# A planned encoder kernel: POOL held to the planned order on its shared SBUF path, later landings in the plan, and a last pass by token tiles

## The chip, the cores and the metric

The kernel runs on one core of a Trainium2 chip. The metric is the device time of one execution in microseconds; the median of three runs stands for a kernel. Engines are named as the profile names them: PE (TensorE), DVE (VectorE), ACT (ScalarE), POOL (GpSimd), SP (SyncE, which issues every DMA here).

## What is computed

A post-norm encoder layer over two sequences, a prompt of 512 tokens and a sample of 1024, width 1024. In float32:

```python
def encoder_layer(x, ...):
    h = x @ w_in                                              # 1024 -> 2048
    c_val, c_gate, r_x, r_gate = split(h, 4)                  # 512 channels each
    c = c_val * sigmoid(c_gate)
    c = silu(layer_norm(depthwise_conv(c, width=31)))         # centred
    rec = (rg_lru(depthwise_conv(r_x, width=4, causal), forward)
           + rg_lru(depthwise_conv(r_x, width=4, anti), reverse)) * gelu(r_gate)
    x = layer_norm(ALPHA * x + concat(c, rec) @ w_out)
    u = depthwise_conv(x @ w_up, width=3)                     # 1024 -> 2 * 2816
    val, gate = split(u, 2)
    f = (gelu(gate) * val) @ w_down                           # 2816 -> 1024
    return layer_norm(ALPHA * x + f)

def encoder_trunk(x, ...):                                    # both sequences
    return encoder_layer(layer_norm(x), ...)
```

`rg_lru` is a gated linear recurrence along the sequence (two small gate products, sigmoid, exp, sqrt, a scan).

## The kernel before

**Products in three terms.** Every product is made of float32r halves: an operand is split into a rounded high part (a copy, mostly on ACT) and a low part (the difference, a TENSOR_TENSOR), and `prod3` multiplies high by high, high by low and low by high. So each weight tile costs a load, an ACT copy and a subtraction on DVE or POOL before PE can use all of it; the low parts of weights that are used again are stored to DRAM and loaded the next time (`weight`).

**Stages.** The prompt and the sample are normed and projected (`ln_in`, `w_in_p`, `w_in_s`). Then a mixer (31-tap convolution and recurrences, work for DVE, ACT and POOL) runs beside a feed-forward pass of another block (work for PE): `mixer_p` beside `w_in_s`; `mixer_s(1)` (second half of the sample) beside `ffn(None)` (prompt), about 360 to 720 us; `mixer_s(0)` beside `ffn(1)`, about 800 to 1040 us; at last `ffn(0)` alone. A feed-forward pass goes over 22 pairs of 128-channel tiles: `up(p)` makes both tiles of a pair, evaluates the 3-tap convolution, gelu and product, and splits the result into one of two buffers `fb`; `down` multiplies a group of pairs by w_down into two PSUM banks in turn (U3 and M2, slot names), and each bank is added to the page `y` by one DVE instruction before PE may write it again. The groups are `GROUPS`: one pair, five times three, two, four.

**Layer norm.** `ln_stats` makes the statistics on DVE and 1/sqrt(var + eps) with one POOL instruction (pow, 128x1, line 197). In the mode "act" a DVE instruction (128x1) makes -mean/std, ACT normalizes, and two TENSOR_TENSOR of 128x1024 apply gain and bias on DVE or POOL ("any"); in the mode "dve" two SCALAR_TENSOR_TENSOR of 128x1024 do all of it.

**What sets the order.** No order is written by hand. Every operation is recorded with reads, writes, an assumed cost and a priority, and `Sched.emit` makes a plan: it lists operations engine by engine, taking at each point the one with the best priority that can start, and the program then issues them in that order. Each engine works through its own queue strictly in that order, waiting by semaphores for data only. For operations marked "any" the plan chooses DVE or POOL. The plan knows that a POOL instruction that reads SBUF and a DVE instruction with two SBUF inputs exclude each other (`takes_port`, `port`), but nothing in the program holds the engines to that: POOL starts when its data is there. A load is planned to be usable when its bytes have passed a modelled bus.

**The last pass, `ffn(0)`.** All pairs but the last are issued in the loop. `last` then issues the last pair's `up`, and the first two token tiles of the last group start with the pairs that are ready and are closed when the last pair is. `body` goes on with token tile 0 and 1 (closing products), a correction row for one page of the other block (`E0`, `a5s`), and tiles 2 and 3; each is normed and stored as 128x1024.

## Time and profile before

| | |
|---|---|
| median of 3 runs | 1616.22 us (1615.35 to 1616.29) |
| the profiled execution | 1616.81 us, of which its span is 1615.0 us |
| PE busy | 1556.7 us, 96% of the span |
| DVE, ACT, POOL busy | 1200.4, 820.3, 188.1 us |
| chain that ended last, by engine | PE 50%, DVE 26%, ACT 10%, DMA 9%, issue 4% |
| matmuls of 128x512 | 6724, 1532.1 us busy in all |

PE is busy nearly all the time, so the time splits into PE's work and the stretches in which PE stands: before its first large product, in short stops in between, and after its last one. A table by stage shows where they are; the stops are read one by one from PE's timeline, and what PE waited for from the table of waits.

### The profile page before, as it was taken

The page shows a single profiled execution, that of the slowest core. Times are in us where ns is not written, and L with a number is a line of the kernel's source. Part 1 is how long each engine was busy: PE and PEld are TensorE (multiplying, and loading weights), DVE is VectorE, ACT ScalarE, POOL GpSimd, SP SyncE. Part 2 cuts the span into 40 slices and gives each one's busy share as a digit, 9 for nine tenths or more (in the row PEclk, how much of TensorE's full clock was granted, in tenths as well). Part 3 has the DMA queues.
Part 4 walks back from the last instruction along what each step waited for, and adds up shares of the span by engine and source line. Part 5 has one row for each costly group of instructions (what it writes and reads, how often), then busy time and mean ns, then how long its engine had stood idle before and what let it go on. Part 6 is the DMA issues. An engine that isn't in the chain of part 4 may idle for free.

```text
span 1615.0 us, 19015 instructions
## 1 busy us (share of the span) xinstructions
PE 1556.7 (96%) x7012; PEld 1281.2 (79%) x7012; DVE 1200.4 (74%) x1867; ACT 820.3 (51%) x1019; POOL 188.1 (12%) x159
## 2 busy tenths in 40 slices
PE   5999999999999999999999999999999999999996
PEld 5887888887778777788888878788887888888784
DVE  8999995498989999873689899844438644545448
ACT  3737775148687974344359833352424433333341
POOL 3102121002122222010101100000001000000003
PEclk9999999999999999999999999999999999999998
DMA  9862335466567455657686676476665556555541
GB/s 359 299 219 96 126 118 187 165 208 206 158 193 223 153 189 190 202 169 248 204 259 201 214 251 202 160 253 200 195 212 196 195 194 195 202 183 195 184 162 65
DMA packets 107517, 316.09 MB, mean 196 GB/s; under 512 B 11936, under 2 KB 12064, under 8 KB 107296
## 3 DMA queue, kind: packets, MB, share of 16 engines
q1 hardware_dynamic: 107424, 314.88, 58.8%
q8 instruction: 55, 0.90, 0.2%
q14 instruction: 38, 0.31, 0.1%
HBM read 247.72 MB, written 67.11 MB: 195 GB/s over the span
## 4 chain that ended last, share of the span: by engine, by line
PE 50%; DVE 26%; ACT 10%; DMA 9%; issue 4%; SPq 0%; POOL 0%; DVEq 0%; ACTq 0%; POOLq 0%
PE b L258 48%; DVE b L206 15%; DVE b L197 9%; ACT b L236 7%; DMA b<-w_up 6%; ACT L236 3%; PE b L266 1%; DMA b<-mixs_d 1%; DMA b<-w_down 1%; DVE b L708 1%; DMA lo_in_d<-b 1%; DVE b L413 0%; DMA b<-lo_out_d 0%; DMA b<-xp 0%; SPq L247 0%
## 5 line engine op out<-in xcount | busy, mean ns | idle before, releaser
L258 PE MATMUL b<-b,b 128*128 128x512 f32 (+1 forms) x6724 | 1532.1, 389 | 24.5 <-DVE b L197 15.9
L258 PEld LDWEIGHTS b<-b,b 128*128 128x128 f32 x6724 | 1247.8, 189 | 293.6 <-DVE b L197 26.5
L206 DVE SCALAR_TENSOR_TENSOR b<-b,b,b 128x511 f32<-128x511 f32 (+12 forms) x848 | 593.0, 715 | 177.5 <-ACT b L236 156.6
L236 ACT ACTIVATE b<-b 128x1024 fp32r<-128x1024 f32 (+4 forms) x576 | 447.3, 799 | 533.6 <-PE b L258 197.2
L197 DVE TENSOR_TENSOR b<-b,b 128x512 f32<-128x512 f32 (+6 forms) x483 | 396.0, 840 | 122.8 <-ACT b L236 70.4
L236 ACT ACTIVATE b<-b,b 128x512 f32<-128x512 f32 (+1 forms) x337 | 256.9, 784 | 220.9 <-PE b L258 160.3
L197 POOL TENSOR_TENSOR b<-b,b 128x1 f32<-128x1 f32 (+3 forms) x89 | 113.6, 1282 | 674.1 <-DVE b L220 443.7
L236 ACT ACT_TABLE_LOAD x106 | 136.0, 1283 | 26.7 <-DVE b L206 23.9
L197 POOL TENSOR_TENSOR b<-b 128x512 f32<-128x512 f32 x52 | 73.3, 1409 | 609.1 <-ACT b L236 597.6
L206 DVE SCALAR_TENSOR_TENSOR b<-b,b 128x512 f32<-128x512 f32 (+2 forms) x81 | 53.6, 673 | 62.5 <-PE b L258 61.8
L413 DVE BATCH_NORM_STATS2 b<-b 128x6 f32<-128x512 f32 x84 | 56.7, 688 | 12.1 <-PE b L266 6.7
L197 DVE TENSOR_TENSOR b<-b 128x512 f32<-128x512 f32 (+3 forms) x80 | 46.5, 600 | 25.8 <-ACT b L236 24.9
L206 DVE SCALAR_TENSOR_TENSOR b<-b 128x512 f32<-128x512 f32 (+1 forms) x110 | 56.0, 518 | 6.8 <-POOL b L197 3.4
L266 PE MATMUL b<-b,b 128*128 128x128 f32 x288 | 40.0, 281 | 17.9 <-DVE b L206 12.1
L266 PEld LDWEIGHTS b<-b,b 128*128 128x128 f32 x288 | 34.8, 145 | 23.9 <-DVE b L206 10.7
L708 DVE TENSOR_TENSOR_SCAN b<-b 128x512 f32<-128x512 f32 x24 | 29.3, 1223 | 0.7
L1046 POOL MEMSET b<- 128x128 f32 x1 | 0.2, 207 | 134.6 <-PE b L258 134.6
L220 DVE TENSOR_SCALAR b<-b 128x1 f32<-128x1 f32 (+1 forms) x61 | 10.3, 171 | 1.7
L415 DVE BATCH_NORM_AGGREGATE b<-b 128x2 f32<-128x12 f32 (+1 forms) x48 | 9.5, 199 | 0.9
L243 DVE COPY b<-b 128x2 f32<-128x2 f32 x44 | 6.6, 150 | 0.0
L220 DVE TENSOR_SCALAR b<-b,b 128x512 f32<-128x512 f32 x2 | 0.9, 484 | 0.0
L900 POOL MEMSET b<- 128x1 f32 x8 | 0.3, 99 | 1.0 <-PE b L258 1.0
(11 smaller groups left out, 1.6 us busy)
## 6 DMA issues: line engine op xcount, KB each, us to landing
b<-w_up SPq DMA_DIRECT2D x132, 512.0 KB, 4.4
b<-lo_up_d SPq DMA_DIRECT2D x88, 512.0 KB, 4.2
b<-w_down SPq DMA_DIRECT2D x132, 256.0 KB, 4.0
lo_up_d<-b SPq DMA_DIRECT2D x44, 512.0 KB, 5.1
b<-lo_down_d SPq DMA_DIRECT2D x88, 256.0 KB, 3.5
b<-w_in SPq DMA_DIRECT2D x32, 512.0 KB, 5.2
b<-w_out SPq DMA_DIRECT2D x24, 512.0 KB, 4.4
lo_down_d<-b SPq DMA_DIRECT2D x44, 256.0 KB, 5.3
```

Of the source, the lines that this page charges most:

```text
L197: return self.op(eng, cost if eng == "any" else cost[eng], lambda e=eng: self.engine(e).tensor_tensor(out=out(), in0=a(), in1=b(), op=op), ...
L206: o = self.op("dve", cost, lambda: self.nc.vector.scalar_tensor_tensor(out=out(), in0=a(), scalar=s() if isinstance(s, View) else s, in1=b ...
L220: return self.op(eng, cost, lambda: e.tensor_scalar(out=out(), in0=a(), scalar1=f(s1), scalar2=f(s2), op0=op0, **({"op1": op1} if op1 is n ...
L236: self.nc.scalar.activation(out=out(), in_=a(), func=func, **k)
L243: return self.op("dve", cost, lambda: self.nc.vector.tensor_copy(out(), a()), [a], [out], prio)
L258: self.nc.tensor.matmul(out=out(), lhsT=a(), rhs=b(), start=start and i == 0, stop=stop and i == len(pairs) - 1)
L266: self.nc.tensor.transpose(o(), i(), ident())
L413: S.op("dve", c.n * 1.0417 + 69, lambda i=i, c=c: nc.vector.bn_stats(out=sm_[6 * i:6 * i + 6](), in_=c()), [c], [sm_[6 * i:6 * i + 6]], prio)
L415: S.op("dve", 211, lambda: nc.vector.bn_aggr(out=sm_[12:14](), in_=sm_[0:6 * n]().rearrange("p (a b) -> p a b", a=n)), [sm_[0:6 * n]], [sm ...
L708: S.op("dve", out.n * 2.0833 + 69, lambda: nc.vector.tensor_tensor_scan(out=out(), data0=a(), data1=b(), initial=0.0, op0=ALU.mult, op1=AL ...
L900: S.op("pool", 100, lambda z=z: nc.gpsimd.memset(z.f32(), 0.0), [], [z], ev)
L1046: S.op("pool", 200, lambda: nc.gpsimd.memset(E0.all.f32(), 0.0), [], [E0.all], 60)
```

## The change

Six edits. (1) The plan remembers which DVE operation took the shared path last (`holder`); a POOL operation that takes it next gets a semaphore wait on that DVE operation (`add_manual_dep`), and in the plan it is ready only a signal's time after it. This concerns 105 POOL instructions; where another wait of POOL already implies it, no wait is added in the program. (2) A load counts as landed 1.4 us later in the plan (`LAND`). (3) The instruction that makes -mean/std moves from DVE to POOL (37 of them, TENSOR_SCALAR). (4) `ffn(0)` has three buffers `fb` in place of two; all 22 pairs are issued in the loop; the last two groups are left to the end. (5) The last group is finished token tile by token tile, eight banks in turn. (6) The last token tile is normed and stored in halves of 128x512. Since the plan is made anew, the order of all engines moves a little everywhere.

```diff
+LAND = 1400.0
-        port = 0.0
+        port, holder = 0.0, None
...
         def ready_on(o, e):
             rt = o.rt.get(e, 0.0)
-            return max(rt, port) if takes_port(o, e) else rt
+            if not takes_port(o, e):
+                return rt
+            return max(rt, port + (LAT["dve", "pool"] if e == "pool" and holder is not None else 0.0))
...
             if takes_port(o, e):
                 port = t + cost
+                if e == "pool":
+                    o.after = holder
+                holder = o if e == "dve" else None
             if e == "sp":
                 bus = max(bus, t + 1500) + o.nbytes / 360.0
-                o.end = bus
+                o.end = bus + LAND
...
         for o in order:
-            if o.both:
-                o.fn(o.eng)
-            else:
-                o.fn()
+            o.ins = o.fn(o.eng) if o.both else o.fn()
+            if o.after is not None:
+                self.tc.add_manual_dep(o.ins.ins, o.after.ins.ins.name, mybir.DependencyInfo(
+                    mybir.DependencyClass.Sync, mybir.DependencyReason.DATA), reason="port")
...
-            S.stt(s_[16:17], mean, -1.0, rstd, ALU.mult, ALU.mult, prio)
+            S.ts("pool", s_[16:17], mean, rstd, ALU.mult, -1.0, ALU.mult, prio=prio - 1.5)
...
-        fb = [S.buf("A0", [2, 2, 512], f32r), S.buf("A1", [2, 2, 512], f32r)]
+        fb = [S.buf(n, [2, 2, 512], f32r) for n in (("A0", "A1", "GB") if blk == 0 else ("A0", "A1"))]
...
+        late = len(GROUPS) - (2 if blk == 0 else 1)
         for gi, grp in enumerate(GROUPS):
             for p in grp:
-                if blk == 0 and p == NPAIR - 1:
-                    break
                 up(p)
-            if gi < len(GROUPS) - 1:
+            if gi < late:
                 down(gi, grp)
...
+            down(late, GROUPS[late], None, PR + 0.2105)
+            wdslot = rot(["G2", "A5", "GW", "A6"])
+            return wds(grp), grp, products
...
     for i in range(4):
         for nh in range(2):
-            b = bank[nh, i]
-            S.mm(b.all, products(get, nh, i, grp[-1:] if i < 2 else grp), i >= 2, True, 70.21 + 0.01 * i)
+            b = S.buf(names(), [512], psum=True)
+            S.mm(b.all, products(get, nh, i, grp), True, True, 70.22 + 0.01 * i)
             yv = y0[i // 2][i % 2, nh * 512:(nh + 1) * 512]
             S.tt("dve", yv, yv, b.all, ALU.add, 6)
...
+    s_ = sm("s")
+    mean, rstd = ln_stats(page_of(y0[1], 1)["halves"], s_, 5.5)
+    for nh in range(2):
+        c = slice(nh * 512, (nh + 1) * 512)
+        x = y0[1][1, c]
+        S.stt(x, x, mean, gb2b[0].buf[0, c], ALU.subtract, ALU.mult, 6)
+        S.stt(x, x, rstd, gb2b[0].buf[1, c], ALU.mult, ALU.add, 6)
+        S.dma(lambda c=c: out_s[384:512, c], x, 256 * 1024, [x], [], 6)
```

**Order, first place: POOL at the start of the program.** `128x1` is the pow of a token tile (b_105 to b_109, tile by tile), `128x1024` the low part of one of the first four w_in tiles (b_82 to b_85). Before:

```order
L197 TENSOR_TENSOR b_106<-b_106,b_116 128x1 [waits DVE_49]
L197 TENSOR_TENSOR b_82<-b_97,b_82 128x1024 [waits DMAHW4_49,Activation_49]
L197 TENSOR_TENSOR b_83<-b_98,b_83 128x1024 [waits DMAHW6_49,Activation_49]
L197 TENSOR_TENSOR b_107<-b_107,b_116 128x1 [waits DVE_49]
L197 TENSOR_TENSOR b_84<-b_99,b_84 128x1024 [waits DMAHW0_49,Activation_49]
```

After:

```order
L200 TENSOR_TENSOR b_106<-b_106,b_116 128x1 [waits DVE_49]
L200 TENSOR_TENSOR b_82<-b_97,b_82 128x1024 [waits DMAHW4_49,Activation_49]
L200 TENSOR_TENSOR b_107<-b_107,b_116 128x1 [waits DVE_49]
L200 TENSOR_TENSOR b_83<-b_98,b_83 128x1024 [waits DMAHW6_49,Activation_49]
L200 TENSOR_TENSOR b_108<-b_108,b_116 128x1 [waits DVE_49]
```

The second weight's low part now stands behind the pow of token tile 2, and that pow waits for a DVE instruction of the same tile which DVE issues after its last instruction for token tile 1.

**Second place: DVE in `ffn(None)` beside `mixer_s(1)`,** at the sum into page y (b_2068 before, b_2065 after) that frees bank U3 for PE. `128x1024` are low parts of weights, `128x511` taps of the 3-tap convolution, `128x512` with b_101 taps of the 31-tap one; L708 is the scan. Before:

```order
L197 TENSOR_TENSOR b_3040<-b_2914,b_3040 128x512
L206 SCALAR_TENSOR_TENSOR b_2914<-b_2978,b_101,b_2914 128x511 x2
L206 SCALAR_TENSOR_TENSOR b_2885<-b_2885,b_2855 128x1
L708 SCALAR_TENSOR_TENSOR b_2885<-b_2885 128x512
L206 SCALAR_TENSOR_TENSOR b_4219<-b_2555,b_101,b_4219 128x512
L197 TENSOR_TENSOR b_4589<-b_4516,b_4589 128x1024
L206 SCALAR_TENSOR_TENSOR b_2914<-b_2864,b_101,b_2914 128x511 x2
L197 TENSOR_TENSOR b_2068<-b_2068,b_3052 128x512
```

After:

```order
L200 TENSOR_TENSOR b_3042<-b_2913,b_3042 128x512
L209 SCALAR_TENSOR_TENSOR b_2913<-b_2983,b_101,b_2913 128x511 x2
L209 SCALAR_TENSOR_TENSOR b_4392<-b_2555,b_101,b_4392 128x512
L200 TENSOR_TENSOR b_4610<-b_4514,b_4610 128x1024
L200 TENSOR_TENSOR b_2065<-b_2065,b_3072 128x512
L209 SCALAR_TENSOR_TENSOR b_2913<-b_2863,b_101,b_2913 128x511
```

The sum stands ahead of the two 128x511 taps that it stood behind, and the scan (21 instructions earlier now) is no longer between.

**Third place: the end of `ffn(0)`,** DVE from the last token tile's second-last sum on (128x512 TENSOR_TENSOR waiting for PE). b_7119 before and b_7121 after hold token tiles 2 and 3, b_8111 tiles 0 and 1. Before:

```order
L197 TENSOR_TENSOR b_7119<-b_7119,b_11629 128x512 [waits PE_49]
L197 TENSOR_TENSOR b_8111<-b_8111,b_7884 128x1024 [waits Activation_49]
L413 BN_STATS b_11643<-b_7119 128x6 [waits DVE_49]
L415 BN_AGGR b_11643<-b_11643 128x2 [waits DVE_49]
L220 TENSOR_SCALAR b_11643<-b_11643 128x1 [waits DVE_49]
L197 TENSOR_TENSOR b_8111<-b_8111,b_7884 128x1024
L197 TENSOR_TENSOR b_7119<-b_7119,b_7884 128x1024 [waits Activation_49]
L197 TENSOR_TENSOR b_7119<-b_7119,b_7884 128x1024 [waits DVE_49]
L206 SCALAR_TENSOR_TENSOR b_7119<-b_7119,b_11643,b_7884 128x1024
L206 SCALAR_TENSOR_TENSOR b_7119<-b_7119,b_11643,b_7884 128x1024 [waits DVE_49,Pool_49]
```

After:

```order
L200 TENSOR_TENSOR b_7121<-b_7121,b_11637 128x512 [waits PE_49]
L422 BN_STATS b_11656<-b_7121 128x6 [waits DVE_49]
L200 TENSOR_TENSOR b_7121<-b_7121,b_7892 128x1024 [waits Activation_49]
L200 TENSOR_TENSOR b_7121<-b_7121,b_7892 128x1024 [waits DVE_49]
L424 BN_AGGR b_11656<-b_11656 128x2
L223 TENSOR_SCALAR b_11656<-b_11656 128x1 [waits DVE_49]
L209 SCALAR_TENSOR_TENSOR b_7121<-b_7121,b_11656,b_7892 128x512 x2
L209 SCALAR_TENSOR_TENSOR b_7121<-b_7121,b_11656,b_7892 128x512 [waits Pool_49]
L209 SCALAR_TENSOR_TENSOR b_7121<-b_7121,b_11656,b_7892 128x512 [waits DVE_49]
```

Two of the four 128x1024 multiplications behind the last sum have moved ahead of it. On POOL in this pass (six products of gelu and value in a row before, one now):

```order
L197 TENSOR_TENSOR b_4841<-b_4841,b_7884 128x1024 [waits DMAHW0_49,DVE_49]
L197 TENSOR_TENSOR b_9238<-b_9238 128x512 [waits Activation_49] x6
L197 TENSOR_TENSOR b_11545<-b_11545,b_116 128x1 [waits DVE_49,Pool_49]
L197 TENSOR_TENSOR b_8111<-b_8111,b_7884 128x1024 [waits DMAHW6_49,DMAHW5_49,DMAHW7_49,PE_49,Activation_49]
L197 TENSOR_TENSOR b_11579<-b_11579,b_116 128x1 [waits DVE_49,Pool_49]
```

After:

```order
L200 TENSOR_TENSOR b_4742<-b_4742,b_7892 128x1024 [waits DMAHW3_49,DVE_49,Activation_49]
L200 TENSOR_TENSOR b_9246<-b_9246 128x512 [waits DVE_49]
L200 TENSOR_TENSOR b_11511<-b_11511,b_116 128x1 [waits DVE_49]
L223 TENSOR_SCALAR b_11511<-b_11511 128x1 [waits Pool_49]
L200 TENSOR_TENSOR b_8114<-b_8114,b_7892 128x1024 [waits DMAHW5_49,Activation_49]
```

The other five products stand in DVE's queue.

## Rows read from the trace of the kernel before

**Rows 1.** By stage, us: length, busy PE, PEld, DVE, ACT, POOL, clock, DMA

```profile
0.00:40.00 40.00, 22.50 (x161) 21.43 (x162) 33.57 (x49) 12.96 (x16) 15.36 (x18) 1.00 0.95 359
...
360.00:720.00 360.00, 346.31 (x1492) 279.84 (x1491) 330.74 (x444) 242.45 (x299) 71.76 (x49) 0.99 0.59 189
720.00:1240.00 520.00, 512.92 (x2308) 422.51 (x2307) 359.72 (x587) 248.69 (x297) 36.99 (x43) 1.00 0.65 214
1240.00:1560.00 320.00, 317.85 (x1394) 260.93 (x1393) 162.76 (x309) 117.21 (x158) 10.16 (x7) 1.00 0.58 193
```

**Rows 2.** Waits, 360 to 720 us: us in total, times, longest

```profile
PE b L258 <- DVE b L197: 8.1, 10, 3.4
```

**Rows 3.** PE's timeline: start, us, instructions, idle before and its releaser

```profile
449.92 72.32 PE L258 MATMUL b<-b,b 128*128 128x512 f32 x311 [1.37 <-POOL b L197]
601.88 30.47 PE L258 MATMUL b<-b,b 128*128 128x512 f32 x126 [3.42 <-DVE b L197]
1029.60 20.71 PE L258 MATMUL b<-b,b 128*128 128x512 f32 x90 [1.40 <-DVE b L197]
```

**Rows 4.** DVE by shape, 360 to 720 us: count, busy us, mean ns, idle

```profile
L197 DVE TENSOR_TENSOR b<-b,b 128x1024 fp32r<-128x1024 f32 x58 | 73.3, 1274 | 16.3 <-ACT b L236 13.5 <-DMA lo_up_d<-b 2.1 <-DMA b<-w_down 0.3
L206 DVE SCALAR_TENSOR_TENSOR b<-b 128x512 f32<-128x512 f32 x48 | 34.0, 721 | 0.3
...
L206 DVE SCALAR_TENSOR_TENSOR b<-b,b,b 128x510 f32<-128x510 f32 x10 | 8.5, 846 | 0.2
L206 DVE SCALAR_TENSOR_TENSOR b<-b,b,b 128x506 f32<-128x506 f32 x3 | 2.2, 745 | 0.0
```

**Rows 5.** The same view, 800 to 920 us

```profile
L197 DVE TENSOR_TENSOR b<-b,b 128x1024 f32<-128x1024 f32 x10 | 12.1, 1219 | 0.5 <-ACT b L236 0.4
L206 DVE SCALAR_TENSOR_TENSOR b<-b 128x512 f32<-128x512 f32 x13 | 8.7, 685 | 0.3 <-ACT b L236 0.3
```

**Rows 6.** By shape, whole span, POOL and one DVE form

```profile
L197 POOL TENSOR_TENSOR b<-b,b 128x512 fp32r<-128x512 f32 x24 | 36.2, 1511 | 176.5 <-ACT b L236 161.0 <-PE b L258 15.0 <-POOL b L197 0.4
L197 POOL TENSOR_TENSOR b<-b,b 128x1 f32<-128x1 f32 x48 | 35.2, 734 | 448.3 <-DVE b L220 443.7 <-DVE b L206 4.7
L206 DVE SCALAR_TENSOR_TENSOR b<-b 128x1 f32<-128x1 f32 x37 | 5.6, 154 | 4.1 <-POOL b L197 3.4
```

**Rows 7.** DVE's and PE's timeline in the first 31 us

```profile
15.15 3.13 DVE L206 SCALAR_TENSOR_TENSOR b<-b,b,b 128x1024 f32<-128x1024 f32 x1
20.20 7.51 PE L258 MATMUL b<-b,b 128*128 128x256 f32 x48
25.72 5.33 DVE L206 SCALAR_TENSOR_TENSOR b<-b,b,b 128x1024 f32<-128x1024 f32 x3
```

**Rows 8.** Waits of PE, 1240 to 1560 us, and DVE's and POOL's timeline there

```profile
PE b L258 <- DVE b L197: 2.1, 6, 0.5
...
1356.90 1.26 DVE L197 TENSOR_TENSOR b<-b 128x1 f32<-128x1 f32 x1 [0.72 <-ACT b L236]
...
1356.85 1.29 POOL L197 TENSOR_TENSOR b<-b 128x512 f32<-128x512 f32 x1 [48.38 <-ACT b L236]
```

**Rows 9.** The chain that ended last, its end: start, us, what

```profile
1589.86 9.31 PE b L258 x41
...
1599.19 1.82 DVE b L197 x2
1601.01 0.61 DVE b L413
...
1602.05 3.40 DVE b L197 x2
1605.47 3.24 DVE b L197
1608.72 1.21 DVE b L206
...
1610.03 1.28 DVE b L206
```

More of the change, by code (lines that the diff above doesn't have):

```diff
@@ L128 @@
 class Op:
-    __slots__ = ("i", "eng", "cost", "fn", "prio", "preds", "succs", "np", "rt", "end", "tab", "nbytes", "start", "both", "shared")
+    __slots__ = ("i", "eng", "cost", "fn", "prio", "preds", "succs", "np", "rt", "end", "tab", "nbytes", "start", "both", "shared", "after", "ins")
 LAT = {("act", "dve"): 142, ("act", "pe"): 227, ("act", "pool"): 170, ("act", "act"): 143,
@@ L136, with __init__ @@
 LOOK = 160
+LAND = 1400.0
 ACT_TABLE = {AF.Sigmoid: "s", AF.Tanh: "sge", AF.Gelu_apprx_tanh: "g", AF.Sqrt: "q", AF.Silu: "u", AF.Exp: "e"}
 class Sched:
-    def __init__(self, nc, sbuf_pool, psum_pool):
+    def __init__(self, tc, sbuf_pool, psum_pool):
+        nc = tc.nc
+        self.tc = tc
         self.nc, self.sbuf_pool, self.psum_pool = nc, sbuf_pool, psum_pool
@@ L272, in emit @@
         for o in ops:
-            o.succs, o.np, o.rt, o.start = [], len(o.preds), {}, None
+            o.succs, o.np, o.rt, o.start, o.after = [], len(o.preds), {}, None, None
         for o in ops:
@@ L367, in body @@
     ps = ctx.enter_context(tc.tile_pool(name="ps", bufs=1, space=PSUM))
-    S = Sched(nc, sb, ps)
+    S = Sched(tc, sb, ps)
     f32, f32r = F32, F32R
@@ L716, in conv_norm @@
         mean, rstd = ln_stats([bk.all], s_, prio)
-        S.stt(s_[16:17], mean, -1.0, rstd, ALU.mult, ALU.mult, prio)
+        S.ts("pool", s_[16:17], mean, rstd, ALU.mult, -1.0, ALU.mult, prio=prio - 1.5)
         for j0, j1, z in z_of:
@@ L932, in up @@
             S.tt("pool" if blk is None else "any", va[p % 2, 0, r], va[p % 2, 0, r], va[p % 2, 1, r], ALU.mult, ev)
-            f = fb[(p // 2) % 2]
+            f = fb[(p // 2) % len(fb)]
             split(f[p % 2, 0, r], f[p % 2, 1, r], va[p % 2, 0, r], ev, lo_eng="dve")
@@ L964, in products @@
                 wh, wl = w[0, ci * 512:(ci + 1) * 512], w[1, ci * 512:(ci + 1) * 512]
-                f = fb[(p // 2) % 2]
+                f = fb[(p // 2) % len(fb)]
                 fh, fl = f[p % 2, 0, i * 128:(i + 1) * 128], f[p % 2, 1, i * 128:(i + 1) * 128]
@@ L968, in products, with down @@
             return pairs
-        def down(gi, grp, banks=None):
+        def down(gi, grp, banks=None, pr=None):
             get = wds(grp)
-            pr = PR + (grp[-1] + 0.5) * 0.01
+            pr = pr or PR + (grp[-1] + 0.5) * 0.01
             for nh in range(2):
@@ L996, in last @@
                 return
-            pr = PR + 0.2101
-            names = rot(["M2", "C0", "C1", "M3", "U3", "U0", "U1", "U2"])
-            nonlocal wdslot
-            wdslot = rot(["A2", "A3", "G2", "A5"])
-            up(NPAIR - 1)
-            get = wds(grp)
-            bank = {}
-            for i in range(2):
-                for nh in range(2):
-                    bank[nh, i] = S.buf(names(), [512], psum=True)
-                    S.mm(bank[nh, i].all, products(get, nh, i, grp[:-1]), True, False, pr)
-            for i in range(2, 4):
-                for nh in range(2):
-                    bank[nh, i] = S.buf(names(), [512], psum=True)
-            return bank, get, grp, products
+            down(late, GROUPS[late], None, PR + 0.2105)
+            wdslot = rot(["G2", "A5", "GW", "A6"])
+            return wds(grp), grp, products
         return last
@@ L1041, in body @@
     last_0 = ffn(0, x1b, y0, 70.0, 6, 64)
-    bank, get, grp, products = last_0()
-    E0 = S.buf("A6", [128], f32r)
+    get, grp, products = last_0()
+    E0 = S.buf("idn", [128], f32r)
     S.op("pool", 200, lambda: nc.gpsimd.memset(E0.all.f32(), 0.0), [], [E0.all], 60)
@@ L1049, in body @@
     a5s = S.buf("A7", [2, 1024], f32r)
-    split(a5s[0], a5s[1], a5.all, 5)
+    names = rot(["C0", "C1", "M3", "U3", "M2", "U0", "U1", "U2"])
     for i in range(4):
+        pg = y0[i // 2][i % 2]
         for nh in range(2):
-            b = bank[nh, i]
-            S.mm(b.all, products(get, nh, i, grp[-1:] if i < 2 else grp), i >= 2, True, 70.21 + 0.01 * i)
+            b = S.buf(names(), [512], psum=True)
+            S.mm(b.all, products(get, nh, i, grp), True, True, 70.22 + 0.01 * i)
             yv = y0[i // 2][i % 2, nh * 512:(nh + 1) * 512]
             S.tt("dve", yv, yv, b.all, ALU.add, 6)
-        if i == 1:
+        if i == 0:
+            split(a5s[0], a5s[1], a5.all, 5)
+        if i < 3:
+            ln2(page_of(y0[i // 2], i % 2), gb2b, "s", 5 + 0.1 * i, out_s[i * 128:(i + 1) * 128, :], "act",
+                "pool" if i == 0 else "any")
+        if i == 0:
             for nh in range(2):
-                b = S.buf("M2" if nh == 0 else "C0", [512], psum=True)
+                b = S.buf(names(), [512], psum=True)
                 c = slice(nh * 512, (nh + 1) * 512)
@@ L1063, in body @@
                 S.tt("dve", yv, yv, b.all, ALU.add, 7)
[L1064 to L1066 removed]
+            ln2(page_of(y1[0], 0), gb2b, "s", 5.05, out_s[512:640, :], "act", "any")
+    s_ = sm("s")
[6 more added lines that the diff above has]
+        S.dma(lambda c=c: out_s[384:512, c], x, 256 * 1024, [x], [], 6)
     with tc.manual_schedule():
```

4 lines of the change are left out of this document (1 added, 3 removed).

## The prediction

> **What bounds the kernel now.** I read the table by stage first [rows 1]. PE is busy 1556.7 of the 1615.0 us span, so no edit here can win more than the time in which PE stands or runs slowly. PE loses 17.5 us before 40 us, 13.7 us between 360 and 720, 7.1 us between 720 and 1240, 2.2 us between 1240 and 1560, and, from the chain, everything behind its last product, which ends at 1599.2 us: 15.8 us [rows 9].
>
> Why PE stands in 360 to 720 us: the waits name DVE's line 197, 8.1 us in ten stops [rows 2]. The longest is 3.42 us at 601.88 [rows 3]. There the second product of a PSUM bank waits for DVE's sum out of that bank, a 128x512 instruction that stood in DVE's queue behind work that was late; the order pieces show the queue (second place). DVE is busy 330.7 of these 360 us, so lateness is not made up quickly. What makes it late is in the shapes: a 128x1024 subtraction takes 1274 ns here and its like 1219 ns in a calmer stretch; a one-scalar 128x512 form 721 against 685; the 128x510 taps 846 against 745 for 128x506 [rows 4, 5]. Those averages hide a few instructions that more than double: one 128x1024 instruction took 3.13 us at 15.15 us, where the same shape takes 1.28 at the end of the program [rows 7, 9]. A one-element instruction shows the cause best: 1.26 us at 1356.90, started 0.05 us after a POOL instruction of 1.29 us, and ended with it [rows 8]. So a DVE instruction that reads SBUF twice stands while POOL is inside one that reads SBUF, for the whole of it.
>
> **The change part by part.** The sum is made against the profiled execution, 1616.8 us.
>
> POOL waits for the planned DVE instruction, and later landings: 360 to 720 us. The three groups above give 58 x 0.055 = 3.2, 48 x 0.036 = 1.7 and 10 x 0.10 = 1.0 us of DVE time stood behind POOL, 5.9 us; the other shapes add perhaps half as much, an estimate. Taken away where POOL had run ahead of the plan, this lets DVE's queue run earlier by that much before the stop at 601.88, and the sum itself has moved forward by two taps of 0.75 us. The landings do the same from ACT's side: the plan no longer puts an ACT copy where its load has not come. I take the stops before DVE's line 197, 8.1 us, as gone. Bounds: nothing (the lateness has other causes), and all 13.7 us plus what the clock costs behind long stops: after 601.88, 126 products took 242 ns each against 233 ns for 311 after 449.92 [rows 3], some 1.1 us in that run, 3 us over the stretch by estimate; 16.7 us. I take 8, since the stops that DVE leads are the ones with a mechanism. **-8.0.**
>
> 720 to 1240 us: 7.1 us idle, of which the stop at 1029.60 is 1.40 us and of the same kind [rows 3]. **-1.5**, bounds 0 and -7.1.
>
> -mean/std on POOL: DVE loses 37 x 0.154 = 5.7 us of work over the whole span [rows 6], little of it where DVE binds. POOL gains 37 instructions that no row shows. The nearest below is DVE's own 154 ns, the nearest above the POOL pow of the same 128x1 shape, 734 ns on average with the waits for the path in it. I take 0.4 us; each lies between pow and an ACT instruction in chains that PE doesn't wait for, except in the last tiles. **0**, bounds -0.5 and +1.
>
> The Trainium skill speaks against this edit: Perfetto Trace Analysis, section "Optimizing Scalar/DVE Operations", says that moving work between VectorE and GpSimd may not help because they share a read port. By it the 37 moves would return nothing; by the rows the instruction removed is 0.154 us on the busier engine; the sum has 0 either way.
>
> The start. DVE's 128x1024 instruction at 15.15 us stood 3.13 - 1.28 = 1.85 us; three at 25.72 took 5.33 instead of 3.84, 1.5 us more [rows 7]. In the new order the second weight's low part on POOL comes behind the pow of tile 2, so behind the instruction that stood (first place). PE's first large product at 20.20 waits through transposes for that instruction. **-1.7**, bounds 0 (the low parts of the next three weights are later by several us, and PE's products want them) and -3.3.
>
> 1240 to 1560 us: the one-element instruction (L206 f5 product, line 197) runs into POOL's product, and DVE's sums behind it let PE stand, 2.1 us in six stops [rows 8]. Five of the six products moved to DVE, half of a 1.22 us instruction each by estimate, with DVE half idle (162.8 of 320 us). **-1.5**, bounds 0 and -2.1.
>
> The end. Behind PE's last product DVE now does one sum and four 128x1024 multiplications, 1.82 + 3.40 + 3.24 = 8.46 us, two of them beside POOL [rows 9]. With the sum at half of a 1219 ns instruction (an estimate, 0.6), the four cost 7.9 us. After the change two are left, with POOL empty: 2 x 1.22 = 2.4. That is 5.4 us less. Statistics, and the last two full-width instructions in four halves, stay, plus two starts, 0.2 us. The pow of the last tile stood under multiplications; now it can start only between halves, and about 0.6 us of it show. The store is half as large, which I put at 0. Tiles 0 and 1 and the other block's page are done before, and the last-but-one group's 48 products (48 x 0.23 = 11 us) cover the last pair's gelu and split. **-4.6**, bounds -3 (tile 2's multiplications arrive late through ACT) and -6.
>
> Sum: 8.0 + 1.5 + 0 + 1.7 + 1.5 + 4.6 = 17.3, so 1599.5 us profiled; the median of the runs lies 0.6 below the profiled execution: **1599 us.**
>
> **Rivals.** (a) *Only the ends gain.* The replanned queues lose elsewhere what the stops in 360 to 1240 give back: a list made by priorities moves everything, and a new order has its own late sums. Then 1.7 + 1.5 + 4.6 = 7.8: 1608 us. For it: DVE stays above 90% busy in 360 to 720, and the next late instruction is then simply another. Against: what made DVE late is mostly named, and the plan now counts it.
>
> (b) *POOL's halves come late, and it is slower.* Each of the 24 low parts that POOL makes for the gate products [rows 6] now waits for a DVE instruction; DVE is late in this stretch, and PE's queue, in order, stops before the gate product. The trace has one such stop: 1.37 us at 449.92, released by POOL [rows 3]. At 1.37 us each, 13 of 24 eat the 17.3 us; all 24 cost 33 us: 1632 us. For it: these waits are real (105 instructions), and the wait is for an engine 92% busy. Against: POOL's product stood for a running DVE instruction before, too, and PE stands once for POOL so far.
>
> (c) *The waits change little.* The one-element row shows that the path is held for a whole POOL instruction [rows 8]. Where the plan itself puts POOL first, a DVE instruction that is early still stands behind it for up to the 1.3 us of that row; a wait helps only where POOL ran ahead of the plan. If most of the 5.9 us is of the planned kind, 360 to 720 gives about 2 from the landings alone, 720 to 1240 nothing: 1616.8 - 2 - 7.8 - 0.6 = 1606 us. For it: the rows don't say in which order the plan had the two. Against: the first place shows one case where it turned them round. The Trainium skill has this as a rule: in SBUF — State Buffer, section "SBUF: two separate sides", the shared pair of ports is an exclusive lock that goes to whoever starts first; the one-element row agrees (1.26 us).
>
> **How the numbers follow.** Forecast (1593 to 1604): 0.48. (a) and (c) together (1604 to 1612): 0.28. More than the forecast, the idle time of 360 to 1240 mostly gone (1587 to 1593): 0.06. Within 0.2% of before, 1613 to 1619.4, about what a measurement can tell from no change: 0.08. Slower, (b): 0.10. So faster 0.82, same 0.08, slower 0.10. The range leaves out the slow side above 1611 and little below 1589: 1589 to 1611.
>
> **What would show it.** Right: the stage 360 to 720 has PE busy at least 353 us for the same work and DVE's 128x1024 mean falls toward 1220 ns; no DVE instruction of one element above 0.3 us after 1240; PE's first large product before 19 us; the span ends 11 to 12 us behind PE's last product. Wrong: stops of PE released by POOL's line 200 (rival b); the same 8 us of stops before DVE's sums with shorter DVE instructions (a); DVE instructions still above 1.7 us beside POOL (c).

## The result, and the profile after

The changed kernel takes 1586.78 us, the median of four runs (1585.08 to 1589.80), against 1616.12 us before (four runs, 1615.35 to 1616.29): ratio 0.9817, 95% interval 0.9801 to 0.9833. That is 29.3 us less. The direction was as forecast, the size was not: 1599 was predicted, with 1589 as the low end.

The profiled execution is 1589.8 us (span 1588.0), the slowest of the four; every row of the kernel after is from it. First the windows by stage, the view of [rows 1] (length, busy time of PE, PEld, DVE, ACT, POOL, clock, DMA):

```profile
0.00:40.00 40.00, 24.75 (x180) 23.85 (x181) 32.79 (x52) 15.12 (x19) 14.73 (x22) 1.00 0.97 374
...
360.00:720.00 360.00, 358.39 (x1587) 293.99 (x1586) 331.81 (x449) 249.23 (x309) 64.68 (x54) 1.00 0.62 200
720.00:1240.00 520.00, 512.68 (x2281) 421.91 (x2280) 359.71 (x581) 239.84 (x288) 33.89 (x56) 0.99 0.66 215
1240.00:1540.00 300.00, 300.00 (x1325) 248.47 (x1325) 153.87 (x304) 115.47 (x158) 1.29 (x1) 1.00 0.60 193
```

Between 360 and 720 us PE now stands 1.6 us instead of 13.7, and gets through 95 products more (1587 against 1492); at 358.39 / 1587 = 0.226 us each that is 21.5 us. Between 720 and 1240 us it does 27 fewer than before: there something was lost. From 1240 to 1540 us it never stands.

The waits of PE from 360 to 720 us (total, times, longest), the view of [rows 2]:

```profile
PE b L261 <- DVE b L200: 1.0, 3, 0.5
PE b L261 <- DVE b L209: 0.4, 1, 0.4
PE b L269 <- ACT b L239: 0.2, 1, 0.2
```

From the table of waits of the kernel before in this stretch, besides the line of [rows 2]:

```profile
ACT b L236 <- DMA b<-w_up: 28.4, 12, 5.7
...
PE b L258 <- ACT b L236: 2.7, 5, 1.1
...
PE b L258 <- DVE b L206: 1.5, 1, 1.5
PE b L258 <- POOL b L197: 1.4, 1, 1.4
```

Ten stops of 8.1 us before DVE's sums have become three of 1.0; of the 2.7 us for ACT 0.2 are left, of the 1.5 us for DVE's line 206 0.4, and the stop for POOL has gone. ACT's own waits for the up weights are now

```profile
ACT b L239 <- DMA b<-w_up: 8.1, 5, 3.1
```

DVE by shape in the same stretch, answering [rows 4] (count, busy us, mean ns, idle):

```profile
L200 DVE TENSOR_TENSOR b<-b,b 128x1024 fp32r<-128x1024 f32 x60 | 73.5, 1233 | 4.7 <-ACT b L239 4.3
...
L209 DVE SCALAR_TENSOR_TENSOR b<-b 128x512 f32<-128x512 f32 x48 | 33.2, 703 | 1.1 <-ACT b L239 0.6
...
L209 DVE SCALAR_TENSOR_TENSOR b<-b,b,b 128x510 f32<-128x510 f32 x10 | 7.5, 748 | 0.2
```

1274, 721 and 846 ns have become 1233, 703 and 748. The idle time before the subtractions went from 16.3 us, 13.5 of it for ACT, to 4.7, 4.3 of it for ACT: DVE waits much less for ACT's copies. POOL by shape over the whole span, answering [rows 6]:

```profile
L200 POOL TENSOR_TENSOR b<-b,b 128x512 fp32r<-128x512 f32 x24 | 30.9, 1296 | 186.1 <-ACT b L239 99.2 <-DVE b L209 51.1 <-DVE b L200 35.8
L200 POOL TENSOR_TENSOR b<-b,b 128x1 f32<-128x1 f32 x48 | 26.4, 550 | 840.8 <-DVE b L223 542.9 <-DVE b L209 284.9 <-DVE b L200 12.7
...
L223 POOL TENSOR_SCALAR b<-b 128x1 f32<-128x1 f32 x37 | 9.9, 267 | 12.2 <-DVE b L200 8.7 <-DVE b L424 0.8
```

The low parts fell from 1511 to 1296 ns and the pow from 734 to 550: POOL stands before its instructions now and not inside them: DVE was the last to release it for 86.9 us before the low parts, where [rows 6] show none, while all its idle time before them grew only from 176.5 to 186.1 us. The new instructions for -mean/std take 267 ns.

The stage that lost, PE's timeline (start, length, products, idle before and its releaser):

```profile
725.82 43.75 PE L261 MATMUL b<-b,b 128*128 128x512 f32 x179 [3.26 <-DMA b<-lo_out_d]
```

A stop of 3.26 us before a load. In the kernel before this place had one of 0.95 us. At the start, answering [rows 7], and at the end, answering [rows 9], DVE and POOL behind PE's last run of products:

```profile
18.85 4.79 PE L261 MATMUL b<-b,b 128*128 128x256 f32 x24
...
1559.69 16.48 PE L261 MATMUL b<-b,b 128*128 128x512 f32 x72
```

```profile
1577.33 0.67 DVE L200 TENSOR_TENSOR b<-b,b 128x512 f32<-128x512 f32 x1
...
1578.64 2.47 DVE L200 TENSOR_TENSOR b<-b,b 128x1024 f32<-128x1024 f32 x2
...
1582.82 0.55 POOL L200 TENSOR_TENSOR b<-b,b 128x1 f32<-128x1 f32 x1 [5.80 <-DVE b L209]
1583.41 1.41 DVE L209 SCALAR_TENSOR_TENSOR b<-b,b,b 128x512 f32<-128x512 f32 x2 [0.67 <-POOL b L200]
```

PE's first large product starts at 18.85 us (20.20 before). Its last run ends at 1576.2, and the span 11.8 us behind it (15.8 before); two full-width multiplications stand there, 2.47 us, instead of four, the last three of which alone took 3.40 + 3.24 = 6.64 us.

**Time by stage.** To compare kernels I note when PE has streamed the same number of product columns that it had streamed in the kernel before at 40, 360, 720 and 1240 us and at its end; differences between these give what each stage gained (minus) or lost. A second measure is DVE time stood beside POOL: of each DVE instruction that overlaps a POOL TENSOR_TENSOR, what it took above the fastest twentieth of its kind (same operation, operand shapes and types), if over 80 ns. In the kernel before it is 31.1 us in all, 9.2 of it in 360 to 720 us. In the table, the column "products" is PE's count in the window 360 to 720 us, "loads" is ACT's time there waiting for the up weights (w_up), "POOL" is DVE time stood beside POOL there. The ratio is against the kernel before as it ran beside each group of kernels; its median there lay between 1614.95 and 1617.4 us, so times of different groups compare to about 2 us. The stages are those of one execution each, and executions of the kernel before ran from 1611.5 to 1619.2 us: a difference of 1 or 2 us in a stage says little. (`last_only` issues the same operations in the same order as the kernel before until after 1200 us, and its stages up to there agree with it to 0.6 us.)

| kernel | ratio, 95% | to 40 | 40-360 | 360-720 | 720-1240 | 1240 to PE's end | behind PE | products | loads | POOL |
|---|---|---|---|---|---|---|---|---|---|---|
| before | 1 | | | | | | | 1492 | 28.4 | 9.2 |
| after | 0.9817 (0.9801-0.9833) | -2.3 | -1.6 | -20.5 | +4.8 | -3.3 | -4.0 | 1587 | 8.1 | 2.5 |
| land_only | 0.9874 (0.9859-0.9889) | +0.1 | +0.1 | -18.6 | +0.8 | -3.4 | 0 | 1581 | 9.8 | 5.9 |
| waits_only | 0.9884 (0.9867-0.9900) | -2.6 | -2.5 | -9.8 | -1.7 | -3.0 | +1.1 | 1542 | 18.6 | 2.5 |
| no_wait | 0.9898 (0.9882-0.9914) | -3.0 | +2.0 | -9.6 | +0.7 | -3.3 | -5.1 | 1537 | 5.5 | 15.2 |
| land_0 | 0.9902 (0.9887-0.9917) | -2.5 | -1.7 | -8.7 | +5.6 | -2.4 | -4.0 | 1537 | 19.2 | 2.4 |
| last_only | 0.9985 (0.9973-0.9997) | +0.3 | 0 | -0.3 | -0.6 | -0.5 | -3.8 | 1494 | 28.2 | 9.4 |
| nmr_dve | 0.9815 (0.9790-0.9839) | -2.7 | -2.4 | -20.9 | +2.6 | -3.3 | -3.1 | 1589 | 6.4 | 4.2 |
| look_150 | 1.0049 (1.0030-1.0069) | +0.3 | -0.6 | +8.3 | -1.0 | +0.1 | 0 | 1466 | 27.4 | 13.7 |
| look_170 | 1.0006 (0.9996-1.0015) | +0.2 | +1.6 | +1.0 | -1.0 | -1.2 | 0 | 1486 | 30.0 | 9.7 |
| land_look150 | 0.9932 (0.9917-0.9946) | +0.1 | -0.7 | -9.1 | +1.8 | -3.4 | 0 | 1543 | 10.4 | 15.4 |
| after_look150 | 0.9814 (0.9799-0.9828) | -2.6 | -1.7 | -15.4 | -4.3 | -3.3 | -4.1 | 1571 | 12.1 | 1.9 |
| land_2800 | 0.9874 (0.9847-0.9901) | -2.7 | -1.6 | -18.5 | +7.1 | -3.3 | -4.0 | 1580 | 5.6 | 3.8 |
| pages_late | 0.9775 (0.9760-0.9790) | -2.4 | -2.5 | -21.3 | -4.9 | -3.3 | -3.1 | 1590 | 6.8 | 4.2 |

### The profile page after: what moved, and what is told of

It reads as the page before. It is cut to its first block, busy times and chain, and to the rows that moved or that the text cites. A ratio compares the mean times of both kernels' runs of the same rounds, so it can differ in the third digit from the quotient of the medians.

```text
span 1588.0 us, 19059 instructions
## 1 busy us (share of the span) xinstructions
PE 1551.1 (98%) x7012; PEld 1282.0 (81%) x7012; DVE 1183.7 (75%) x1841; ACT 811.0 (51%) x1013; POOL 159.9 (10%) x187
## 4 chain that ended last, share of the span: by engine, by line
PE 78%; DVE 10%; ACT 6%; DMA 2%; issue 2%; POOL 0%; SPq 0%; DVEq 0%; POOLq 0%; ACTq 0%
PE b L261 76%; DVE b L209 5%; DVE b L200 4%; ACT b L239 4%; ACT L239 2%; PE b L269 2%; DMA b<-w_up 1%; DMA b<-lo_out_d 1%; DVE b L717 0%; DMA b<-xp 0%; DMA b<-lo_down_d 0%; POOL b L200 0%; DVE b L422 0%; SPq L250 0%; DVE b L424 0%
## 5 line engine op out<-in xcount | busy, mean ns | idle before, releaser
L209 DVE SCALAR_TENSOR_TENSOR b<-b,b,b 128x511 f32<-128x511 f32 (+11 forms) x850 | 588.7, 706 | 166.7 <-ACT b L239 143.5
L200 DVE TENSOR_TENSOR b<-b,b 128x512 f32<-128x512 f32 (+5 forms) x487 | 393.0, 826 | 121.0 <-ACT b L239 68.4
L200 POOL TENSOR_TENSOR b<-b,b 128x1 f32<-128x1 f32 (+2 forms) x85 | 88.2, 1043 | 1064.7 <-DVE b L223 542.9
L209 DVE SCALAR_TENSOR_TENSOR b<-b,b 128x512 f32<-128x512 f32 (+2 forms) x81 | 50.2, 633 | 67.0 <-PE b L261 66.4
L200 POOL TENSOR_TENSOR b<-b 128x512 f32<-128x512 f32 x47 | 60.8, 1295 | 337.8 <-ACT b L239 154.7
L200 DVE TENSOR_TENSOR b<-b 128x512 f32<-128x512 f32 (+3 forms) x85 | 43.5, 528 | 21.5 <-ACT b L239 20.7
L209 DVE SCALAR_TENSOR_TENSOR b<-b 128x512 f32<-128x512 f32 (+1 forms) x73 | 49.7, 691 | 3.8 <-ACT b L239 2.8
L223 POOL TENSOR_SCALAR b<-b 128x1 f32<-128x1 f32 x37 | 9.9, 267 | 12.2 <-DVE b L200 8.7
```

The costliest lines, as they stand in the source:

```text
L200: return self.op(eng, cost if eng == "any" else cost[eng], lambda e=eng: self.engine(e).tensor_tensor(out=out(), in0=a(), in1=b(), op=op), ...
L209: o = self.op("dve", cost, lambda: self.nc.vector.scalar_tensor_tensor(out=out(), in0=a(), scalar=s() if isinstance(s, View) else s, in1=b ...
L223: return self.op(eng, cost, lambda: e.tensor_scalar(out=out(), in0=a(), scalar1=f(s1), scalar2=f(s2), op0=op0, **({"op1": op1} if op1 is n ...
```

## The experiments

The theory from the result: DVE's queue in 360 to 720 us was late from two sides, POOL inside the shared path and ACT's copies standing in the plan where their load had not come; either side makes the sums late that free PE's banks, and the change takes away both. Rival one: POOL's waits do it, as the prediction had it, and the landings are small. Rival two: a new order alone does it, since any of these edits reshuffles the whole program.

**Waits taken out, order kept.** `no_wait` is the changed kernel with its plan and its order, without the semaphore waits of POOL. In the traces PE, DVE, ACT, POOL and SP go through the same sequence of operations and shapes in both.

```diff
-            if o.after is not None:
+            if False:
```

> The changed kernel with its plan and its order of every engine left as they are, and only the semaphore waits of POOL on DVE taken out of the program. Theory 1 (POOL running ahead of the plan is what makes DVE late, and the waits themselves cure it): DVE instructions of more than 1.7 us beside POOL come back, PE's lost time in 360 to 720 us goes from about 3 us back to 12 or more, and the time is 1600 us or more. Theory 2 (the order planned with later landings does it; the lock of the path does the rest alone): within 3 us of the changed kernel, 1584 to 1590 us.

1600.38 us: 13.6 more than the changed kernel. DVE time stood beside POOL grows from 4.4 to 25.9 us over the span and from 2.5 to 15.2 in 360 to 720 us, and that stage gives back 10.9 us of its 20.5. Not everything that came with edit (1) hangs on the semaphores: up to 40 us this kernel gains 3.0 us without them, so there it is the new order alone; behind PE's last product it is 1.0 us quicker than the changed kernel (10.8 us against 11.8). What a collision looks like, DVE's and then POOL's timeline of this kernel:

```profile
436.81 2.09 POOL L200 TENSOR_TENSOR b<-b,b 128x512 fp32r<-128x512 f32 x1 [5.25 <-issue]
```

```profile
437.67 1.78 DVE L209 SCALAR_TENSOR_TENSOR b<-b,b,b 128x511 f32<-128x511 f32 x1
```

The tap takes 1.78 us where one takes 0.75, because POOL (2.09 us, 1.30 alone) had started into the instruction ahead of it. PE's waits show where that ends:

```profile
PE b L261 <- DVE b L200: 6.3, 9, 1.3
...
PE b L261 <- ACT b L239: 3.4, 3, 1.8
```

The waits matter in this order. ACT's waits for loads stay small (5.5 us), so the two sides are separate.

**Landings taken out of the changed kernel.**

```diff
-LAND = 1400.0
+LAND = 0.0
```

> The changed kernel with a landing of 0 in the plan in place of 1.4 us, all else kept. Theory 2 (landings): ACT copies stand before their loads again, DVE and PE follow; most of the 20 us of 360 to 720 us is lost again, 1600 us or more. Theory 1 (waits): 1585 to 1592 us.

1601.65 us, 14.9 more than the changed kernel. DVE is hardly held by POOL (2.4 us in 360 to 720), yet ACT waits 19.2 us for w_up there, and the sums stop PE again:

```profile
ACT b L239 <- DMA b<-w_up: 19.2, 8, 5.7
...
PE b L261 <- DVE b L200: 6.2, 8, 1.6
```

**Each edit alone on the kernel before.** `waits_only` adds edit (1), `land_only` edit (2).

```diff
+                if e == "pool":
+                    o.after = holder
+                holder = o if e == "dve" else None
...
+            if o.after is not None:
+                self.tc.add_manual_dep(o.ins.ins, o.after.ins.ins.name, mybir.DependencyInfo(
...
```

> The kernel before with the waits of POOL in the planned order alone (the plan's rule for them with it). Theory 1: PE's lost time in 360 to 720 us falls from 22 to under 8 us, the end and the plan's landings stay as before: 1596 to 1602 us. Theory 2: 1610 to 1616 us.

1597.95 us. The time is within 1596 to 1602; PE's lost time in 360 to 720 us fell by 9.8 us from 22, not to under 8 as expected, about half of what the whole change gains there. The start (-2.6 us) is wholly edit (1)'s, since `land_only` has 0 there, and by `no_wait` it is the order that comes with the edit. From 40 to 360 us it is the semaphores: -2.5 us here and +2.0 in `no_wait`. What is left in 360 to 720 us is ACT's side:

```profile
ACT b L238 <- DMA b<-w_up: 18.6, 7, 5.6
...
PE b L260 <- DVE b L199: 6.0, 8, 1.5
```

```diff
+LAND = 1400.0
-                o.end = bus
+                o.end = bus + LAND
```

> The kernel before with the later landings in the plan alone. Theory 2: 1594 to 1602 us. Theory 1: 1609 to 1616 us, POOL still runs ahead and single DVE instructions still take 1.7 us and more.

1596.49 us: 1.4 us of plan constant is worth as much as all of POOL's waits with the order that comes with them. In 360 to 720 us it gains 18.6 of the 20.5 us, with the collisions mostly still there (5.9 of 9.2 us):

```profile
ACT b L237 <- DMA b<-w_up: 9.8, 6, 3.9
...
PE b L259 <- DVE b L198: 1.7, 4, 0.8
```

The loads themselves mostly did not go out sooner: counted in PE's products, the 39 loads of up weights of 360 to 700 us are issued by the median 4 products (about 1 us) earlier in `land_only` than in the kernel before, single ones up to 60, and at the same point in the changed kernel. So the later place of the copies is the likelier part of it; the runs don't separate the two.

Rival one falls. The gains don't add: 1.26% for the landings, 1.16% for the waits and 0.15% for the last pass make 2.57%, and the whole change has 1.83%. In 360 to 720 us 18.6 + 9.8 us is more than all that PE lost there (22.2 us, below): both work on the same lateness.

**Is it only a new order?** Two controls change nothing but `LOOK`, by how many ns the plan may look past its present time for something better to issue. The order moves everywhere; no wait and no landing is added.

```diff
-LOOK = 160
+LOOK = 150
```

> The kernel before with one number of the plan changed that says nothing of the chip (how far ahead of the first possible start it looks for a better operation, 150 in place of 160 ns): a new order of the same kind. Theory 2 (what counts is that landings or waits are right): PE's lost time in 360 to 720 us stays within 4 us of the 22 before, 1612 to 1620 us. Theory 3 (the order before was an unlucky one, and almost any other is better): 5 us or more are gone from that stage, under 1610 us.

1622.22 us, 2 us above the range, and the stage 360 to 720 us loses 8.3 us, twice what was allowed for. ACT waits 27.4 us for w_up and DVE stands 13.7 us beside POOL:

```profile
ACT b L236 <- DMA b<-w_up: 27.4, 14, 6.3
PE b L258 <- DVE b L197: 8.3, 11, 3.1
```

> The kernel before, with only the look-ahead of the plan changed (LOOK 160 to 170): the whole order moves, no wait is added and no landing is planned later. It is the second control for what a new order alone is worth; the first one (LOOK 150) came out 8 us worse in 360 to 720 us. Theory L (the edits act by what they say): 1612 to 1625 us, with ACT waiting 20 to 30 us for the up weights in 360 to 720 us and DVE's sums still stopping PE there for 5 us or more. Rival R (the order of before was an unlucky one, and most replannings win): below 1605 us.

1616.7 us (ratio 1.0006): no difference; ACT waits 30.0 us for w_up, and DVE's sums stop PE for 13.4 us. So an order made anew by itself moved this stage by +8.3 and +1.0 us. Neither gained what the edits gain; but two orders are few, and a single kernel's stage can be off by several us for its order alone. Hence the same edits in the other order:

> The kernel before with the later landings alone (LAND 1400), and the look-ahead at 150. The same two orders without the landings gave 1615 to 1617 (160) and 1622 (150). If the later landing is what saves PE in 360 to 720 us, it does so in this order too: 1594 to 1606 us, and ACT waits less than 15 us for the up weights there (27 us in the order of 150 without it). Rival: the gain of the landings was one lucky order, and this one comes out at 1610 to 1622 us, with stops of PE before DVE's sums of 8 us or more.

1604.86 us, within 1594 to 1606. Against `look_150` the landings take off 17.4 us, in the stage 360 to 720 us 8.3 + 9.1 = 17.4 as well; in the other order it was 18.6. ACT's waits for w_up fall from 27.4 to 10.4 us again, while DVE still stands 15.4 us beside POOL:

```profile
ACT b L237 <- DMA b<-w_up: 10.4, 8, 2.5
```

> The changed kernel with the look-ahead at 150. If its gain comes from its edits and not from one order: 1583 to 1596 us, less than 6 us of DVE time lost beside POOL, PE busy at least 354 us in 360 to 720 us. If half of it was the order: 1597 to 1606 us, with PE busy about 350 us in 360 to 720 us.

1585.84 us: the changed kernel's time is the same in these two orders. With 1.9 us beside POOL in the stage, the other edits, the waits among them, add 6.3 us to what the landings give there (15.4 - 9.1); in the order of 160 they add 1.9 (20.5 - 18.6), where `land_only` had 5.9 us of collisions and `land_look150` 15.4. Rival two falls for the total in the orders tried; how the gain of this one stage divides between waits and landings depends on the order, and no single number for either is right.

**The last pass alone.** `last_only` has edits (4) to (6) on the kernel before.

> The kernel before with the edits of the last pass alone (three buffers, last group token tile by token tile, last tile in halves); waits, landings and -mean/std as before. Theory (the terms of the prediction): the end 4 to 5 us shorter, stages before 1240 us within 1 us of before, 1240 to 1560 within 1 us: 1611 to 1613 us. Rival (the end's gain is mostly the work of POOL's waits, since two of the slow instructions there stood beside POOL): 1614 to 1616 us.

1613.38 us, ratio 0.9985, 0.9973 to 0.9997: a gain of some 2.4 us, less than expected. By its profile, from one of the quicker of its ten executions, PE ends 1.1 us earlier and the span 3.8 us less behind it.

**-mean/std left on DVE.**

```diff
-            S.ts("pool", s_[16:17], mean, rstd, ALU.mult, -1.0, ALU.mult, prio=prio - 1.5)
+            S.stt(s_[16:17], mean, -1.0, rstd, ALU.mult, ALU.mult, prio)
...
```

> The changed kernel with -mean/std left on DVE. Theory (37 instructions of 0.15 us matter only where DVE binds, in few places): within 3 us of the changed kernel, 1584 to 1590 us. Rival (DVE's queue standing before each of them until POOL's pow is done made it late): 1592 us or more.

1585.38 us against 1586.78; the two ratios' intervals lie over each other. The move is worth nothing that can be measured.

**A larger landing.** `LAND` at 2800 in the changed kernel.

> The changed kernel with a landing of 2.8 us in the plan, twice the change's. Theory 2 (the plan is right when its landing is the chip's, 4.4 us from issue with 1.4): the plan now puts ACT copies later than needed, PE waits for weights that are there, 1588 to 1598 us. Theory 2b (what helps is slack before ACT copies, more is no worse): 1580 to 1588 us, ACT's waits for loads under 5 us in 360 to 720 us.

1593.76 us, slower by 7 than with 1400. The stage 360 to 720 us is 2 us worse although ACT waits only 5.6 us for w_up; 720 to 1240 us loses 7.1 us, by stops of another kind:

```profile
PE b L261 <- ACT b L239: 5.7, 3, 2.8
PE b L269 <- DVE b L200: 2.4, 1, 2.4
```

What is planned later than it lands comes late too. With 1400 the plan has a 512 KB load that meets no queue usable 1.5 + 1.46 + 1.4 = 4.4 us after its issue, and 4.4 us is the median landing of the up weights in the kernel before; with 2800 it is 5.8.

**The stop that the change made larger.** Before the 3.26 us stop SP's timeline in the changed kernel is:

```profile
716.12 0.33 SPq L250 DMA_DIRECT2D b<-w_out  x1
716.61 0.80 SPq L250 DMA_DIRECT2D b<-x0s_d  x2
717.51 0.38 SPq L250 DMA_DIRECT2D b<-lo_out_d  x1
```

The load that PE stops for, the low part of the residual's second weight, is issued at 717.51, behind two 512 KB loads of a page (x0s_d) that only the sums after the products need; it releases PE at 725.82, 8.3 us later, while the DMA engines were 95% busy from 712 to 728 us. `pages_late` is `nmr_dve`, where the same stop is 4.09 us, with those page loads recorded behind the second weight's products:

```diff
-        for i in range(4):
-            S.load(t[i // 2][i % 2], x0_d[seq][4 * half + i], prio - 1, r=[k_x0[seq][4 * half + i]])
...
+                if nh == 0 and kp == 1:
+                    for i in range(4):
+                        o = S.load(t[i // 2][i % 2], x0_d[seq][4 * half + i], prio - 1, r=[k_x0[seq][4 * half + i]])
+                        o.preds.add(m.i)
```

> The changed kernel with -mean/std left on DVE (1585.4 us), and in the output projection's residual the two loads of a page are recorded behind the products of the second weight, so that they aren't issued ahead of that weight's low part. Theory: PE's stop of 3.3 us at about 726 us, released by the load of that low part, comes from the queue ahead of it and goes: 1580 to 1584 us. Rival: the low part is late because its slot comes free only at 717 us; then the stop shrinks by less than a third and the time stays at 1585 to 1588 us, or a new stop stands before the sums into the page that now comes late.

1579.35 us (1579.30 to 1580.12), ratio 0.9775, 0.9760 to 0.9790: 6.0 us faster than `nmr_dve`, 7.4 faster than the changed kernel, so faster than both kernels of the case, and a little below what was expected. By the traces PE, DVE, ACT and POOL go through the same sequence of operations and shapes as in `nmr_dve`; SP's queue is what differs. SP's and PE's timeline there, and then PE's in `nmr_dve`:

```profile
714.33 0.33 SPq L250 DMA_DIRECT2D b<-w_out  x1
715.15 0.33 SPq L250 DMA_DIRECT2D b<-lo_out_d  x1
...
726.45 2.22 SPq L250 DMA_DIRECT2D b<-x0s_d  x4
```

```profile
709.41 51.95 PE L261 MATMUL b<-b,b 128*128 128x512 f32 x228
```

```profile
725.03 43.35 PE L261 MATMUL b<-b,b 128*128 128x512 f32 x179 [4.09 <-DMA b<-lo_out_d]
```

PE runs through. The rival, a slot that comes free only at 717 us, falls too: the load went out at 715.15. The stop was the queue ahead of the load. It cost more than its length: behind it 179 products took 43.75 / 179 = 244 ns each in the changed kernel and 43.35 / 179 = 242 in `nmr_dve`, here 51.95 / 228 = 228. The granted clock of 720 to 770 us (the third figure from the end of a row), in the changed kernel and then in `pages_late`:

```profile
720.00:770.00 50.00, 46.74 (x197) 38.09 (x196) 15.28 (x23) 11.13 (x12) 2.66 (x4) 0.93 0.71 239
```

```profile
720.00:770.00 50.00, 50.00 (x230) 41.59 (x229) 23.46 (x36) 13.26 (x15) 2.52 (x4) 1.00 0.73 256
```

0.93 is a mean over the levels 2.4 and 1.2 GHz: PE was at the lower one for about a seventh of the 50 us.

`after_look150` agrees: there SP issues no page load between w_out and lo_out_d, the stop is absent, and 720 to 1240 us gains 4.3 us.

## Why the prediction was right or wrong

Term by term, forecast against the profiled executions (27.0 us of span):

| term | forecast (bounds) | measured |
|---|---|---|
| to 40 us | -1.7 (0 to -3.3) | -2.3 |
| 40-360 | none taken | -1.6 |
| 360-720 | -8.0 (0 to -16.7) | -20.5 |
| 720-1240 | -1.5 (0 to -7.1) | +4.8 |
| 1240-1560 | -1.5 (0 to -2.1) | -3.3 |
| end | -4.6 (-3 to -6) | -4.0 |
| -mean/std | 0 (-0.5 to +1) | 0, by `nmr_dve` |

**The step that failed is the price of the stage 360 to 720 us, -8.0, taken from the sentence "I take the stops before DVE's line 197, 8.1 us, as gone".** Those stops did go (1.0 us is left). But the step took this one releaser's share for the value of the whole stage, put the rest at nothing, and had the idle time plus 3 us as the bound; the stage lost 22.2 us and gave 20.5. The time that DVE stood behind POOL, 5.9 us and half as much again, was well sized: the count above gives 9.2. Two things were missed.

First, whose stops they were. PE also stood 2.7 us for ACT, 1.5 for DVE's line 206 and 1.4 for POOL in this stretch. I left these out because the mechanism named only DVE's sums. But an ACT copy that waits for its load, the DVE subtraction that waits for the copy and the sum behind that subtraction are one chain of in-order queues; when the load is planned where it lands, all three kinds of stops go. The evidence was in the rows: 13.5 of the 16.3 us before DVE's subtractions in [rows 4] are idle time for ACT, and ACT's own waits, 28.4 us for w_up, are in the table of waits of which I quoted one line. I gave the later landings a sentence and POOL the arithmetic. The runs turn this round: landings alone -18.6 and -17.4 us in two orders, each against its own order without them; waits alone -9.8, in one order.

Second, slow products, most of them by the clock. I put what they cost behind long stops at 3 us for the stage. By the starts of successive products, against the spacing they have in this trace when nothing holds them (their columns at 2.4 GHz and 15 ns), PE lost 22.2 us there: 16.9 in 18 gaps of over 260 ns, and 6.7 in 46 products that started 60 to 260 ns late (the rest were 1.4 us quicker than that spacing). The granted clock of the kernel before, in the windows that hold the long stops, and of the changed one in the same windows:

```profile
380.00:480.00 100.00, 95.44 (x406) 76.62 (x406) 91.94 (x121) 81.56 (x101) 21.33 (x15) 0.98 0.61 192
...
600.00:720.00 120.00, 114.08 (x493) 92.93 (x494) 105.57 (x149) 50.78 (x62) 16.53 (x13) 0.97 0.59 189
```

```profile
380.00:480.00 100.00, 99.68 (x438) 81.52 (x436) 97.62 (x132) 79.72 (x100) 19.38 (x15) 1.00 0.60 195
...
600.00:720.00 120.00, 119.18 (x540) 98.05 (x539) 97.29 (x134) 53.78 (x66) 12.12 (x15) 1.00 0.66 210
```

In the first, 32 products more fit into the window; 4.24 us are PE's idle time less, and the rest is the same work at 235 against 228 ns. The clock figures of the kernel before, 0.98 of 100 us and 0.97 of 120 us, make some 2 and 3.6 us. The bound of 16.7 should have been about 22.

**720 to 1240 us had the wrong sign.** The part that I named came: the stops before DVE's sums fell from 3.8 us in four to 0.9 in one. But here are PE's waits in this stage, in the kernel before and then in the changed one:

```profile
PE b L258 <- DVE b L197: 3.8, 4, 1.4
...
PE b L258 <- DMA b<-lo_out_d: 0.9, 1, 0.9
```

```profile
PE b L261 <- DMA b<-lo_out_d: 3.3, 1, 3.3
PE b L261 <- DMA b<-lo_down_d: 2.0, 1, 2.0
PE b L261 <- DVE b L200: 0.9, 1, 0.9
...
```

All of them come to 7.1 us, as much as the 7.1 of idle time before, since a load that was 0.95 us late became 3.26 us late. And the stops are fewer and longer, with more slow products behind them: products that started 60 to 260 ns late cost 2.2 us before and 5.2 after. I had asked what the change takes away there, not which load the residual would want while the queue ahead of it stayed the same; the stage begins 24 us sooner for PE. `pages_late` shows that 4.9 us could be had where 4.8 were lost. This loss also hid part of the miss: the sum came out 9.7 us beyond the forecast, and with the -1.5 that was forecast here it would have been 16; that the time lies only 2 us below the range is luck. Not all of it is this one stop: `land_0` loses 5.6 us there with only 1.1 us before that load and 3.5 before DVE's sums; what does that in each order stays open.

**1240 to 1560 us** was mis-sized in the same way, by idle time alone: -3.3 where -2.1 was the bound. Edit (1) and the landings each take it alone (-3.0 and -3.4). **40 to 360 us** was left out of the sum although PE stands 2.0 us there before; it gave 1.6, by the semaphores as `no_wait` shows.

**What came as forecast.** The start: the first large product before 19 us (18.85), by the new place of the second weight's low part, as the prediction had it, and not by the semaphores (`no_wait` starts it at 18.58). The end: 11.8 us behind PE's last product, 11 to 12 were forecast, and DVE stands 0.67 us for the last pow where 0.6 was put. PE busy at least 353 us in 360 to 720 us (358.39). DVE's 128x1024 toward 1220 (1233). No DVE instruction of one element above 0.3 us after 1240 us: its two forms average 212 and 159 ns there, and the longest took 220. -mean/std: nothing; POOL's instruction took 267 ns where I took 0.4 us.

**The rivals.** Rival (b), POOL's halves late: PE has no stop in 360 to 720 us that POOL released, although POOL's low parts waited 86.9 us for DVE; POOL had time to wait. Rival (a), only the ends gain: the middle gained most. Rival (c), the waits change little: `no_wait` has 25.9 us of DVE time beside POOL and the changed kernel 4.4, so in this order most of it is POOL running ahead of the plan. What the Trainium skill says of the exclusive lock (SBUF — State Buffer, section "SBUF: two separate sides") is not touched by this: the 1.78 us tap above agrees with it; the waits let the two meet less. The chances had the outcome near the bottom: 0.06 for 1587 to 1593 us, nothing below.
